# Gate A of a gated decoder block as seven half-size block products, and a layer norm scaled by ScalarE

## The chip, the core and the metric

The kernel runs on one core of one Trainium2 chip. A core has five engines with queues of their own: TensorE (PE) multiplies matrices into PSUM, VectorE (DVE) and ScalarE (ACT) work elementwise, GpSimd (POOL) does elementwise work and issues transfers, SyncE (SP) issues transfers. The metric is device microseconds of one execution; the kernel before takes 796.54 us, the median of three runs (794.74 to 796.85).

## The reference

One decoder block on 512 positions of 1024 channels, all in fp32. What matters here, cut short:

```
z = (rms_norm(x, norm1_g) * (1 + scale1) + shift1) @ w_in      # shift, scale, gate from silu(c) @ w_ada
a_u, a_v, q, k, v, qi, ki, wi, g_a, g_b = split(z)
v    = layer_norm(gelu(a_v), ln_g, ln_b)                       # (4 chunks, 128, 8 groups, 128)
y_a  = gelu(a_u) * (einsum('gts,nsgc->ntgc', tril(w_s), v) + b_s.T)
y_b  = sparse attention: indexer scores from qi, ki, wi; the 128 best keys of each query; softmax
x    = x + gate1 * ((sigmoid(g_a) * (y_a @ w_proj_a) + sigmoid(g_b) * (y_b @ w_proj_b)) @ w_out)
x    = x + gate2 * ((silu(f_g) * f_u) @ w_ffn_out)             # f_g, f_u = split(h2 @ w_ffn_in)
return rms_norm(x, final_norm_g)
```

Gate A is g_a = h @ w_in[:, 4168:5192], a product of 512 x 1024 by 1024 x 1024; projection A is y_a @ w_proj_a.

## The kernel before

Every fp32 product is made of three matmuls in a rounded fp32 format (fp32r): each operand is split into a high part (a copy that rounds) and a low part (the difference), and high x high, high x low and low x high are added in PSUM (L66 to L68). Activations lie transposed, channels on partitions, positions along the free side; h is split once into hT. Weights are streamed in chunks of 128 x 1024 elements (four row blocks by 256 columns): SyncE loads a chunk into one of three raw buffers, ScalarE copies it to one of three hi buffers (L125), and VectorE or GpSimd subtracts to one of three lo buffers (L129; for the u products, gate A and projection A it is GpSimd). get() prepares two chunks ahead of the one that TensorE is at. Into the same stream are put the dots of the modulation: 128 outputs of silu(c) @ w_ada each, a multiply and sum on VectorE over a loaded piece (L199); those of the middle of the kernel share one buffer, mraw.

There is no scheduler: each engine does its instructions in the order in which the program writes them, and semaphores hold an instruction until its operands are there. The order is written as steps. The stages that are touched, with the place of each in time:

- Queries, keys and values (62 to 101 us). q_tasks gives each chunk its side work; at the last but one, ki_stats and ki_norm (L631) normalise the indexer key, TensorE transposes it (L648).
- a_v (to 156 us), then gelu; ws is loaded and masked on VectorE (L834).
- a_u (156 to 205 us) in eight chunks. au_tasks(s) is the side work ahead of chunk s, au_post that behind it: at s = 1 and 2 VectorE scales a_v (L872, L873); from s = 3 TensorE mixes a group (mix_mm) and a step later VectorE adds the bias and multiplies with u (mix_ev: L892, L894), ScalarE and VectorE split the result to yT.
- Gate A and projection A (205 to 294 us), group by group of 256 output columns: two chunks of gate A, whose sigmoid ScalarE writes (ga_evac), two of projection A, whose result VectorE multiplies with it (pa_evac, L974). Between them VectorE works off the top-k of the indexer, 16 rounds of three maxima and three replacements (bg: L698, L702).
- Attention, projection B, output and FFN follow. The FFN is already done by seven half-size block products with summed operands (R: 256 columns); the sums of its weights are made by transfers on GpSimd's queue that add in DRAM.

Of the kernel before, what the change touches and what calls it, by code (L numbers as in the profile page):

```python
# [28 lines left out]
def block_kernel(ctx: ExitStack, tc: tile.TileContext, x, x_t, c_row, positions, w_ada_t, w_first, w_in,  # L29
                 gmlp_ln_g, gmlp_ln_b, gmlp_w_s, gmlp_b_s, w_proj_a, w_proj_b,  # L30
# [44 lines left out]

    def add_w(src, kts, c0, n, lo=None, where=None):
# [8 lines left out]
    def issue(i):  # L85
# [22 lines left out]
    def prep(i):  # L108
# [54 lines left out]
    cols = tiny.tile([128, 80], F32, name="cols")  # L163
    A.dma_start(cols[:, 0:67], small)
# [3 lines left out]
    freq = cols[:, 50:51]  # L168
    bgate = {2: cols[:, 51:59], 5: cols[:, 59:67]}
# [98 lines left out]
    dram = ctx.enter_context(tc.tile_pool(name="dram", bufs=1, space=bass.MemoryType.DRAM))  # L268
# [60 lines left out]
    A.dma_start(ident, consts[:, 0:128])  # L329
# [21 lines left out]
    tiny.tile([128, 96], F32, name="fill")  # L351
# [28 lines left out]
    for cmp, sgn in ((OP.is_gt, -1.0), (OP.is_lt, 1.0)):  # L380
# [7 lines left out]
           "q": mid.tile([128, 2, S], F32, name="tab_q", tag="G3", bufs=1)}  # L388
# [117 lines left out]
    for kt in range(8):  # L506
# [53 lines left out]
    kf = mid.tile([128, 2, S], F32, name="kf", tag="A0", bufs=1)  # L560
# [12 lines left out]
    rqt = [mid.tile([128, S], F32, name="rqt", tag=t, bufs=1) for t in ("P0", "P1", "rq")]  # L573
# [29 lines left out]
    k_hi = mid.tile([128, 2, S], F32R, name="k_hi", tag="k_hi", bufs=1)  # L603
    k_lo = mid.tile([128, 2, S], F32R, name="k_lo", tag="k_lo", bufs=1)

    k_pl = mid.tile([128, 2, 128], F32, name="k_pl")

    def k_b(h):
        split(k_hi[:, h], k_lo[:, h], kf[:, h])
        A.activation(k_pl[:, h], kf[:, h, :128], AF.Copy)  # L610

    v_hi, v_lo = (vmid.tile([128, 4, 256], F32R, name=t, tag=t, bufs=1) for t in ("v_hi", "v_lo"))
    kit = mid.tile([128, 4, 64], F32, name="kit", tag="A1", bufs=1)
# [36 lines left out]
    def ki_a():  # L650
        p = kp[0]
        kr.append(mid.tile([128, S], F32, name="kr", tag="A1", bufs=1))
        A.activation(kr[0], p, AF.Identity, scale=igc, bias=ibc)
        rope_a("ki", kr[0], "i", 128)
# [106 lines left out]
    def idx_mms(n):  # L761
        while iu[0] < 24 and n:
# [5 lines left out]
    QT = {0: [lambda: rows_in(0)],  # L768
          1: [lambda: rows_in(1)],
          2: [lambda: qi_a(0)],  # L770
# [47 lines left out]
    vg = [mid.tile([128, 2, D], F32, name=f"vg{i}", tag=f"P{i}", bufs=1) for i in range(2)]  # L818
    lng = mid.tile([128, D], F32, name="lng", tag="G0", bufs=1)
    lnb = mid.tile([128, D], F32, name="lnb", tag="G1", bufs=1)  # L820
    ws = mid.tile([128, 8, 128], F32, name="ws", tag="A0", bufs=1)
    P.dma_start(lng, rows_bcast(gmlp_ln_g, D))
    P.dma_start(lnb, rows_bcast(gmlp_ln_b, D))
    P.dma_start(ws, gmlp_w_s)
    late = {}

    def load_bs():
        late["bsb"] = mid.tile([128, 8, 128], F32, name="bsb", tag="G3", bufs=1)
# [3 lines left out]
    def ws_mask():  # L832
        late["wmT"] = mid.tile([128, 8, 128], F32, name="wmT", tag="G2", bufs=1)
        V.tensor_tensor(late["wmT"], ws, triu[:, None, :].to_broadcast([128, 8, 128]), op=OP.mult)  # L834

    VT = {0: [lambda: k_b(1)], 2: [lambda: rows_a(1), lambda: rows_b(1)], 4: [lambda: rows_a(2), lambda: rows_b(2)], 6: [load_bs], 7: [ws_mask]}
# [51 lines left out]

    def mix_ev(m):
# [1019 lines left out]
```

## Time and profile before

| | |
|---|---|
| median of 3 runs | 796.54 us |
| the profiled execution | 795.69 us, of which the span is 793.9 us |
| TensorE busy | 782.8 us, mean granted clock 0.997 |
| VectorE, ScalarE, GpSimd busy | 649.7, 424.9, 176.4 us |
| moved by DMA | 144.59 MB, mean 182 GB/s |

An engine's busy time is the sum of its instructions' spans; matmuls overlap in their pipeline, so that TensorE's pace is read from the distance between starts. What bounds the kernel is read from the list of waits and from the chain of waits: the work that ended last, followed back step by step to what released it.

### The profile page before, as it was taken

The page shows a single profiled execution, that of the slowest core. Times are in us where ns is not written, and L with a number is a line of the kernel's source. Part 1 is how long each engine was busy: PE and PEld are TensorE (multiplying, and loading weights), DVE is VectorE, ACT ScalarE, POOL GpSimd, SP SyncE. Part 2 cuts the span into 40 slices and gives each one's busy share as a digit, 9 for nine tenths or more (in the row PEclk, how much of TensorE's full clock was granted, in tenths as well). Part 3 has the DMA queues.
Part 4 walks back from the last instruction along what each step waited for, and adds up shares of the span by engine and source line. Part 5 has one row for each costly group of instructions (what it writes and reads, how often), then busy time and mean ns, then how long its engine had stood idle before and what let it go on. Part 6 is the DMA issues. An engine that isn't in the chain of part 4 may idle for free.

```text
span 793.9 us, 12210 instructions
## 1 busy us (share of the span) xinstructions
PE 782.8 (99%) x4599; PEld 692.8 (87%) x4599; DVE 649.7 (82%) x1093; ACT 424.9 (54%) x757; POOL 176.4 (22%) x206
## 2 busy tenths in 40 slices
PE   8999999999999999999999999999999999999996
PEld 6779988888888888988888899999999999878885
DVE  5985865798899748886697879889999898798887
ACT  6555545423322237665536577555655656576654
POOL 2062224362353411000020000313231222100001
PEclk9999999999999999999999999999999999999998
DMA  9946353432346551148682503989897978565754
GB/s 362 416 155 169 112 191 82 126 92 94 131 150 203 180 186 54 54 133 270 226 244 52 190 1 108 248 256 276 248 273 208 261 192 215 173 200 199 226 182 148
DMA packets 87148, 144.59 MB, mean 182 GB/s; under 512 B 6705, under 2 KB 54593, under 8 KB 86898
## 3 DMA queue, kind: packets, MB, share of 16 engines
q1 hardware_dynamic: 75328, 112.97, 43.1%
q0 software_dynamic: 10864, 29.83, 16.1%
q10 hardware_dynamic: 898, 1.03, 0.4%
q8 instruction: 36, 0.59, 0.3%
q14 instruction: 22, 0.18, 0.1%
HBM read 139.73 MB, written 25.17 MB: 208 GB/s over the span
## 4 chain that ended last, share of the span: by engine, by line
PE 85%; DVE 8%; ACT 3%; DMA 2%; issue 1%; POOL 0%; POOLq 0%; SPq 0%; ACTq 0%; DVEq 0%
PE pb L68 8%; PE pb L67 8%; PE pb L66 8%; PE R L66 7%; PE R L67 7%; PE R L68 7%; PE pfo L67 4%; PE pfo L66 4%; PE pfo L68 4%; PE pgb L66 2%; PE pgb L67 2%; PE pgb L68 2%; PE pav L67 2%; PE pav L66 2%; PE pav L68 2%
## 5 line engine op out<-in xcount | busy, mean ns | idle before, releaser
L125 ACT ACTIVATE hi<-raw 128x1024 fp32r<-128x1024 f32 (+1 forms) x105 | 107.9, 1029 | 90.0 <-PE pb L67 24.2
L129 DVE TENSOR_TENSOR lo<-raw,hi 128x1024 fp32r<-128x1024 f32 (+2 forms) x69 | 80.6, 1169 | 27.9 <-ACT hi L125 27.8
L129 POOL TENSOR_TENSOR lo<-raw,hi 128x1024 fp32r<-128x1024 f32 x29 | 72.8, 2513 | 99.3 <-ACT hi L125 67.9
L66 PE MATMUL pb<-h,hi 128*128 128x512 f32 (+1 forms) x176 | 67.4, 383 | 0.0
L68 PE MATMUL pb<-h,lo 128*128 128x512 f32 (+1 forms) x176 | 66.8, 379 | 0.0
L67 PE MATMUL pb<-h,hi 128*128 128x512 f32 (+1 forms) x176 | 66.8, 379 | 0.0
L67 PE MATMUL pfo<-lo,za 128*128 128x512 f32 (+1 forms) x144 | 55.5, 385 | 0.5 <-DVE lo L129 0.5
L66 PE MATMUL pfo<-hi,za 128*128 128x512 f32 (+1 forms) x144 | 55.4, 384 | 0.0
L68 PE MATMUL pfo<-hi,za 128*128 128x512 f32 (+1 forms) x144 | 55.2, 384 | 0.0
L199 DVE CUSTOM_DVE_ANT_0 mraw<-mraw,scb,cols 128x1024 f32<-128x1024 f32 x27 | 39.3, 1456 | 14.6 <-DMA mraw<-in_w_ada_t_dram 14.6
L321 POOL COPY sm<-sm 128x1 f32<-128x1 f32 x36 | 27.5, 763 | 86.3 <-ACT sm L320 86.3
L66 PE MATMUL R<-tb,sx 128*128 128x256 f32 x160 | 44.7, 280 | 0.3 <-ACT R L1647 0.3
L66 PE MATMUL R<-tb,hi 128*128 128x256 f32 x160 | 44.4, 278 | 0.0
L67 PE MATMUL R<-tb,hi 128*128 128x256 f32 x160 | 44.4, 278 | 0.0
L68 PE MATMUL R<-tb,lo 128*128 128x256 f32 x160 | 44.4, 278 | 0.0
L68 PE MATMUL R<-tb,sx 128*128 128x256 f32 x160 | 44.4, 277 | 0.0
L67 PE MATMUL R<-tb,sx 128*128 128x256 f32 x160 | 44.4, 277 | 0.0
L68 PEld LDWEIGHTS pb<-h,lo 128*128 128x128 f32 x176 | 33.0, 188 | 5.7
L66 PEld LDWEIGHTS pb<-h,hi 128*128 128x128 f32 x176 | 33.1, 188 | 5.5
L67 PEld LDWEIGHTS pb<-h,hi 128*128 128x128 f32 x176 | 33.1, 188 | 5.4
L301 POOL DMA_DIRECT2D wsum<-in_w_ffn_out_dram x24 | 21.3, 889 | 68.7 <-DMA wsum<-wsum 34.7
L67 PEld LDWEIGHTS pfo<-lo,za 128*128 128x128 f32 x144 | 27.1, 188 | 6.6 <-DVE lo L129 1.4
(374 smaller groups left out, 2553.7 us busy)
## 6 DMA issues: line engine op xcount, KB each, us to landing
raw<-in_w_ffn_in_dram SPq DMA_DIRECT2D x44, 512.0 KB, 5.6
raw<-in_w_in_dram SPq DMA_DIRECT2D x38, 512.0 KB, 3.7
wsum<-in_w_ffn_out_dram POOLq DMA_DIRECT2D x30, 512.0 KB, 7.8
mraw<-in_w_ada_t_dram SPq DMA_DIRECT2D x27, 512.0 KB, 3.6
raw<-wsum SPq DMA_DIRECT2D x20, 512.0 KB, 3.7
s<-in_w_ada_t_dram SPq DMA_DIRECT2D x16, 512.0 KB, 8.8
raw<-in_w_ffn_out_dram SPq DMA_DIRECT2D x16, 512.0 KB, 4.4
wsum<-wsum POOLq DMA_DIRECT2D x10, 512.0 KB, 5.3
```

Source lines behind the costliest of these rows:

```text
L66: T.matmul(o, wh, rh, start=start, stop=False, **kw)
L67: T.matmul(o, wh, rlo, start=False, stop=False, **kw)
L68: T.matmul(o, wlo, rh, start=False, stop=stop, **kw)
L125: A.activation(hi[:, :m], e["raw"][:, :m], AF.Copy)
L129: e["lo"].tensor_sub(lo[:, :m], e["raw"][:, :m], f(hi[:, :m]))
L199: V.tensor_tensor_reduce(out=raw[:, o], in0=raw[:, o], in1=c, scale=1.0, scalar=col if o.start else bias, op0=OP.mult, op1=OP.add, accum_o ...
L301: P.dma_start(wsum[n][o], src, accum_op=OP.add)
L321: P.tensor_copy(t, t)
```

## The change

1. Gate A is done in two rounds of 512 output columns. Each is a 2 x 2 block product, (positions halves) x (row halves) times (row halves) x (column halves), made of seven block products of 256 positions, 512 rows and 256 columns instead of eight. Four of the seven need sums of blocks of h (S1 = A21 - A22, S2 = A11 - S1, S3 = S2 - A22, S4 = A12 - S2), and four need sums of blocks of the weights. VectorE makes these sums of h in place in xT, ScalarE and VectorE split them to buffers of their own (h_hi, h_lo). The weight sums are made in DRAM by sixteen transfers on GpSimd's queue, half of them adding (x_move), spread over the query, a_v and a_u chunks. Results are gathered in PSUM: ScalarE seeds one bank from another with a changed sign, or keeps a bank in SBUF, and VectorE adds the kept ones. All low halves of these weights are GpSimd's. Projection A is as before; two groups follow each round.
2. The layer norm of a_v: ScalarE scales (v - mean) * rstd in one pass; the weight ln_g moves into the mixing's evacuation (one pass of VectorE with a scalar), the offset ln_b into the mixing's bias, for which TensorE sums the columns of the mixing weights and VectorE adds eight products of 128 x 128. The mask is put on by GpSimd.
3. Side work moves: the key's split goes to step 27 of 30, the top-k's rounds get a table by step (BG), six of the dots stand among the block products, two stand in each group of projection A, ScalarE's high half of y goes behind the chunk (ylate) and VectorE's low half ahead of the next (ylow). Several tiles change their place in SBUF, and the scratch of software transfers is halved.

```
+    for r in range(2):
+        W_X.append([])
+        for p, b in enumerate((blk(r, 0), xsum[r, 1], xsum[r, 2], blk(r, 3), xsum[r, 3], blk(r, 2), xsum[r, 4])):
+            W_X[r].append(add_w(b, [0, 1, 2, 3], 0, 256, P, 16))
+            if (r, p) in GA_DOTS:
+                add_m(*next(mm_), mid="A2")
+        for g in (2 * r, 2 * r + 1):
+            W_PA.append(group(w_pa, 256 * g, mods=mm_, pool=2, nm=(1, 1)))
...
-          7: [ki_stats, ki_norm],
-          8: [lambda: k_b(0)]}
+          7: [ki_stats, lambda: h_hi("S1"), lambda: h_lo("S1"), lambda: h_lo("S4"), ki_norm]}
...
     def ln_v2(tk):
         v = vg[tk // 2][:, tk % 2]
-        V.scalar_tensor_tensor(v, v, mva[:, tk, 0:1], lng, op0=OP.subtract, op1=OP.mult)
-        V.scalar_tensor_tensor(v, v, rva[:, tk:tk + 1], lnb, op0=OP.mult, op1=OP.add)
+        A.activation(v, v, AF.Identity, scale=rva[:, tk:tk + 1], bias=nmr[:, tk:tk + 1])
...
     def mix_ev(m):
-        V.tensor_tensor(y.rearrange("p (a n) -> p a n", a=4), p.rearrange("p (a n) -> p a n", a=4),
-                        late["bsb"][:, m, None, :].to_broadcast([128, 4, 128]), op=OP.add)
+        V.scalar_tensor_tensor(y.rearrange("p (a n) -> p a n", a=4), p.rearrange("p (a n) -> p a n", a=4),
+                               lngc[:, m:m + 1], late["bsb"][:, m, None, :].to_broadcast([128, 4, 128]),
+                               op0=OP.mult, op1=OP.add)
         V.tensor_mul(y, y, u)
-        split(yT[m][0], yT[m][1], y)
+        def hi():
+            A.activation(yT[m][0], y, AF.Copy)
+            ylow.append(lambda: V.tensor_sub(yT[m][1], y, f(yT[m][0])))
+        ylate.append(hi)
...
+    def xround(r, evac):
...
+        for p, (key, z, start) in enumerate(X_STEPS):
+            hi, lo = get(W_X[r][p])
+            au_tasks()
+            if start:
+                Z[z] = two(bank(z, "zx"))
+            parts = [(j, m, slice(128 * m, 128 * m + 128), h_block(key, j)) for j in range(4) for m in range(2)]
+            for j, m, cc, (hh, hl) in parts:
+                T.matmul(Z[z][:, m], hi[:, j, cc], hh, start=start and j + m == 0, stop=False, skip_group_check=True)
+                T.matmul(Z[z][:, m], hi[:, j, cc], hl, start=False, stop=False, skip_group_check=True)
+            for j, m, cc, (hh, hl) in parts:
+                T.matmul(Z[z][:, m], lo[:, j, cc], hh, start=False, stop=j == 3, skip_group_check=True)
+            if p == 0:
+                seed_(1, 0)
+            elif p == 1:
+                keep_(3)
+            elif p == 2:
+                seed_(2, 1)
+                zlate.append(lambda: V.tensor_add(Z[1], Z[1], kept[3]))
+            elif p == 3:
+                evac(0, Z[0])
+            elif p == 4:
+                keep_(2)
+                zlate.append(lambda: (V.tensor_sub(Z[3], Z[3], kept[2]), evac(3, Z[3])))
...
+    for r in range(2):
+        xround(r, ga_evac(r))
+        for g in (2 * r, 2 * r + 1):
+            opt_b(W_PA[g], 8, yT, ((0, 1), (2, 3), (0, 1), (4, 5))[g], pa_evac(g), au_tasks, au_post)
```

The first place is VectorE's queue at the indexer key (mv and kin are its mean and normalised form, v_lo the values' low half, hs the splits of the sums of h). Before:

```order
L625 BN_AGGR mv<-bst 128x2
L633 TENSOR_SCALAR kin<-kit,mv,sm 128x128 x4
L637 TENSOR_TENSOR v_lo<-pv_793,v_hi 128x256
L637 TENSOR_TENSOR v_lo<-pv_794,v_hi 128x256
L637 TENSOR_TENSOR v_lo<-pv_795,v_hi 128x256
L637 TENSOR_TENSOR v_lo<-pv_796,v_hi 128x256
```

And now:

```order
L696 BN_AGGR mv<-bst 128x2
L676 TENSOR_TENSOR hs<-xT_109,hs 128x1024
L676 TENSOR_TENSOR hs<-xT_110,hs 128x512
L676 TENSOR_TENSOR hs<-xT_110,hs 128x256 x2
L704 TENSOR_SCALAR kin<-kit,mv,sm 128x128 x4
L708 TENSOR_TENSOR v_lo<-pv_811,v_hi 128x256
```

Four low-part passes of S1 and S4 now stand between the key's statistics and its normalisation.

The second place is ScalarE's queue where gate A begins (hi<-raw is the copy of a weight chunk, y the high half of the mixed product, u the gelu of a_u, sg the sigmoid, zx a PSUM bank of the block products, zk a kept one). Before:

```order
L932 ACTIVATE u<-pb 128x512 x2
L363 ACTIVATE y_1506<-y 128x512
L125 ACTIVATE hi<-raw 128x1024
L363 ACTIVATE y_1507<-y 128x512
L125 ACTIVATE hi<-raw 128x1024
L964 ACT_TABLE_LOAD
L964 ACTIVATE sg<-pb 128x512 x2
```

And now:

```order
L1049 ACTIVATE u<-pb 128x512 x2
L981 ACTIVATE y_1532<-y 128x512
L134 ACTIVATE hi<-raw 128x1024
L1105 ACTIVATE zx<-zx 128x512
L981 ACTIVATE y_1532<-y 128x512
L134 ACTIVATE hi<-raw 128x1024
L1109 ACTIVATE zk<-zx 128x512
L981 ACTIVATE y_1533<-y 128x512
L134 ACTIVATE hi<-raw 128x1024
L1105 ACTIVATE zx<-zx 128x512
```

A high half of y stands ahead of each weight copy, as before, but the chunk that the copy is for now feeds half as many columns, and seeding and keeping a bank are added between.

The third place is VectorE's queue between projection A's first and second product with the gate (part is the product, mraw and GG the dots, sco and m the top-k). Before, these stand around the first:

```order
L199 ISA mraw,GG_88<-mraw,scb,cols 128x1024
L199 ISA GG_88 128x1
L974 TENSOR_TENSOR part_1901<-pb,sg 128x512 x2
L702 MATCH_REPLACE sco_637<-m_2064,sco_637 128x512
L702 MATCH_REPLACE sco_636<-m_2066,sco_636 128x384
L702 MATCH_REPLACE sco_635<-m_2068,sco_635 128x256
```

And now, around the second:

```order
L209 ISA mraw,GG_88<-mraw,scb,cols 128x1024
L209 ISA GG_88 128x1
L773 MATCH_REPLACE sco_640<-m_2325,sco_640 128x512
L773 MATCH_REPLACE sco_639<-m_2327,sco_639 128x384
L773 MATCH_REPLACE sco_638<-m_2329,sco_638 128x256
L209 ISA mraw,GG_88<-mraw,scb,cols 128x1024
L209 ISA GG_88 128x1
L1087 TENSOR_TENSOR part_2316<-pb,sg 128x512 x2
```

Seven dots stand in VectorE's queue from the fifth block product of round 0 up to the second product with the gate (five of them ahead of the first); before, one stood ahead of each chunk of gate A and of projection A alike, from the a_u chunks on.

## Rows read from the trace of the kernel before

**Rows 1.** The page: TensorE's busy time; the chain of waits by engine.
```profile
PE 782.8 (99%) x4599; PEld 692.8 (87%) x4599; DVE 649.7 (82%) x1093; ACT 424.9 (54%) x757; POOL 176.4 (22%) x206
...
PE 85%; DVE 8%; ACT 3%; DMA 2%; issue 1%; POOL 0%; POOLq 0%; SPq 0%; ACTq 0%; DVEq 0%
```
**Rows 2.** Waits of TensorE: us in total, times, longest us.
```profile
PE warm L462 <- POOL ones L352: 2.3, 1, 2.3
PE pfo L67 <- DVE lo L129: 0.5, 2, 0.3
```
**Rows 3.** Busy us by stage: PE, PEld, DVE, ACT, POOL, clock, DMA share, GB/s.
```profile
62.00:101.00 39.00, 39.00 (x229) 37.52 (x229) 29.83 (x58) 20.03 (x40) 9.14 (x15) 1.00 0.53 143
...
205.00:294.00 89.00, 89.00 (x403) 73.87 (x402) 69.25 (x151) 24.92 (x31) 34.16 (x15) 1.00 0.56 183
```
**Rows 4.** Timeline of TensorE, 512 columns and mixing: start us, duration us.
```profile
203.42 0.39 PE L66 MATMUL pb<-h,hi 128*128 128x512 f32 x1
203.65 0.39 PE L67 MATMUL pb<-h,hi 128*128 128x512 f32 x1
...
204.10 1.05 PE L886 MATMUL mix<-wmT,vg 128*128 128x128 f32 x8
204.91 0.48 PE L66 MATMUL pb<-h,hi 128*128 128x512 f32 x1
```
**Rows 5.** Timeline of TensorE in the FFN: first and last of twelve.
```profile
539.31 0.28 PE L67 MATMUL R<-h,sx 128*128 128x256 f32 x1
...
540.56 0.28 PE L66 MATMUL R<-tb,sx 128*128 128x256 f32 x1
```
**Rows 6.** Timeline of all engines at the indexer key.
```profile
95.62 2.39 POOL L129 TENSOR_TENSOR lo<-raw,hi 128x1024 fp32r<-128x1024 f32 x1
95.67 3.19 DVE L633 TENSOR_SCALAR kin<-kit,mv,sm 128x128 f32<-128x128 f32 x4 [1.46 <-POOL sm L360]
...
98.78 1.41 DVE L637 TENSOR_TENSOR v_lo<-pv,v_hi 128x256 fp32r<-128x256 f32 x4
...
100.83 0.60 PE L648 MATMUL kiT<-ident,kin 128*128 128x128 f32 x4
```
**Rows 7.** Timeline of GpSimd and VectorE where they meet.
```profile
146.60 2.46 POOL L129 TENSOR_TENSOR lo<-raw,hi 128x1024 fp32r<-128x1024 f32 x1 [5.98 <-ACT hi L125]
...
147.92 2.23 DVE L834 TENSOR_TENSOR wmT<-ws,triu 128x1024 f32<-128x1024 f32 x1
...
160.45 3.25 DVE L873 SCALAR_TENSOR_TENSOR vg<-vg,sm,lnb 128x1024 f32<-128x1024 f32 x1
```
**Rows 8.** Groups by line and shape: busy us, mean ns of one, idle before.
```profile
L873 DVE SCALAR_TENSOR_TENSOR vg<-vg,sm,lnb 128x1024 f32<-128x1024 f32 x4 | 11.1, 2785 | 0.2
L125 ACT ACTIVATE hi<-raw 128x1024 fp32r<-128x1024 f32 x96 | 101.3, 1057 | 84.3 <-PE pb L67 24.2 <-PE pfo L68 11.5 <-issue 11.1
L1331 DVE TENSOR_TENSOR raw<-raw 128x1024 f32<-128x1024 f32 x20 | 24.5, 1226 | 0.7
L894 DVE TENSOR_TENSOR y<-y,u 128x512 f32<-128x512 f32 x8 | 5.5, 692 | 0.3
L363 ACT ACTIVATE y<-y 128x512 fp32r<-128x512 f32 x8 | 5.1, 632 | 28.4 <-DVE y L894 28.4
L364 DVE TENSOR_TENSOR y<-y,y 128x512 fp32r<-128x512 f32 x8 | 5.5, 693 | 5.6 <-ACT y L363 5.6
```
**Rows 9.** Timeline of VectorE: three dots that follow each other.
```profile
243.55 1.28 DVE L199 CUSTOM_DVE_ANT_0 mraw<-mraw,scb,cols 128x1024 f32<-128x1024 f32 x1 [0.60 <-DMA mraw<-in_w_ada_t_dram]
...
248.26 1.33 DVE L199 CUSTOM_DVE_ANT_0 mraw<-mraw,scb,cols 128x1024 f32<-128x1024 f32 x1 [0.45 <-DMA mraw<-in_w_ada_t_dram]
...
253.27 1.72 DVE L199 CUSTOM_DVE_ANT_0 mraw<-mraw,scb,cols 128x1024 f32<-128x1024 f32 x1 [0.69 <-DMA mraw<-in_w_ada_t_dram]
```
**Rows 10.** Transfers by tensor: issues, KB each, median us to landing.
```profile
raw<-in_w_ffn_in_dram SPq DMA_DIRECT2D x44, 512.0 KB, 5.6
raw<-in_w_in_dram SPq DMA_DIRECT2D x38, 512.0 KB, 3.7
```

More of the change, by code (lines that the diff above doesn't have):

```diff
@@ L98, in issue @@
             return
+        if e["where"] == 16:
+            e["view"] = lambda t: t.rearrange("p (j n) -> p j n", j=4)
+            SY.dma_start(raw, e["src"])
+            return
         k0, nk, n = e["kts"][0], len(e["kts"]), e["n"]
@@ new lines, in h_sum, with h_home, four @@
+    def h_sum(key):
+        a, b = {"S1": ("A21", "A22"), "S2": ("A11", "S1"), "S4": ("A12", "S2"), "S3": ("S2", "A22")}[key]
+        V.tensor_sub(h_part(key), h_part(a), h_part(b))
+    def h_home(key):
+        def four(tag, pool=mid):
+            return [(pool.tile([128, 4, 256], F32R, name="hs", tag=tag, bufs=1), 0, 4)]
+        if key == "S1":
+            return four("G0"), four("G1")
+        if key == "S2":
+            return four("G3"), four("gate", base)
+        if key == "S3":
+            return four("G2"), four("k_lo")
+        return four("hs4", base), [(mid.tile([128, 2, 256], F32R, name="hs", tag="rq", bufs=1), 0, 2)] + [
+            (mid.tile([128, 1, 256], F32R, name="hs", tag="qh", bufs=2), 2 + e, 1) for e in range(2)]
@@ new lines, in h_hi, with h_lo, h_block @@
+    def h_hi(key):
+        HS[key] = h_home(key)
+        A.activation(HS[key][0][0][0], h_part(key), AF.Copy)
+    def h_lo(key):
+        hi = HS[key][0][0][0]
+        for t, j, n in HS[key][1]:
+            V.tensor_sub(t, h_part(key)[:, j:j + n], f(hi[:, j:j + n]))
+    def h_block(key, j):
+        if key[0] == "A":
+            o = slice(256 * (key[1] == "2"), 256 * (key[1] == "2") + 256)
+            return tuple(t[:, o] for t in hT[4 * (key[2] == "2") + j])
+        return tuple(next(t[:, j - a] for t, a, n in part_ if a <= j < a + n) for part_ in HS[key])
@@ L901, in au_post @@
     def au_post():
-        for m in AT.get(austep[1], []):
+        s = austep[1]
+        austep[1] += 1
+        if s == 2:
+            rs_mm()
+        for m in AT.get(s, []):
             mix_mm(m)
-        austep[1] += 1
+        while ylate:
+            ylate.pop(0)()
     def au_tasks():
@@ L913, in au_tasks @@
             rstd(rva, mva[:, :, 1], 4, 1.0)
-            run_bg(0.8)
-        elif s == 1:
-            ln_v2(0)
-            ln_v2(1)
-        elif s == 2:
-            ln_v2(2)
-            ln_v2(3)
+            V.scalar_tensor_tensor(nmr, mva[:, :, 0], -1.0, rva, op0=OP.mult, op1=OP.mult)
+        elif s < 3:
+            ln_v2(2 * s - 2)
+            ln_v2(2 * s - 1)
+        elif s == 3:
+            bias_mix()
+        while ylow:
+            ylow.pop(0)()
         for m in AT.get(s - 1, []):
             mix_ev(m)
-        if s > 2:
-            run_bg(1.6 if s < 8 else 2.0)
-        if s in (20, 21):
-            at_split(s - 20)
+        while zlate:
+            zlate.pop(0)()
+        for _ in range(BG.get(s, 0)):
+            run_bg(0.1)
+        if s < 8:
+            x_move()
+        elif s == 8:
+            assert not xm
+        elif s == 27:
+            k_b()
+        if s in (28, 29):
+            at_split(s - 28)
+    BG = {1: 1, 2: 2, 3: 2, 4: 2, 5: 1, 6: 2, 7: 2, 9: 1, 10: 1, 11: 1, 12: 1, 13: 1, 14: 1, 15: 2, 16: 1, 17: 2, 18: 1,
+          19: 1, 20: 1, 21: 1, 22: 1, 23: 1, 24: 1, 26: 2, 27: 1, 28: 1, 29: 1}
+    zlate = []
     def au_evac(g):
@@ L970, in ev @@
         def ev(pb):
+            if not part:
+                part.extend(mid.tile([128, 4, S], F32, name=f"part{i}", tag=f"P{i}", bufs=1) for i in range(2))
             def mul():
@@ new lines, in ga_evac, with ev @@
+    def ga_evac(r):
+        t = {}
+        def ev(z, zb):
+            c, th = z % 2, z // 2
+            if c not in t:
+                t[c] = mid.tile([128, 2, S], F32, name="sg", tag=f"A{c}", bufs=1)
+                for m in range(2):
+                    sig[4 * r + 2 * c + m] = t[c][:, m]
+            A.activation(t[c][:, :, 256 * th:256 * th + 256], zb, AF.Sigmoid)
+        return ev
+    for r in range(2):
+        xround(r, ga_evac(r))
+        for g in (2 * r, 2 * r + 1):
+            opt_b(W_PA[g], 8, yT, ((0, 1), (2, 3), (0, 1), (4, 5))[g], pa_evac(g), au_tasks, au_post)
@@ L1137, in o_w @@
         else:
-            ow[key] = tuple(base.tile([128, 2, S], F32R, name=t, tag=t, bufs=3) for t in ("hi", "lo"))
+            ow[key] = pair((2, S))
         split(*ow[key], oraw[src])
```

168 lines of the change are left out of this document (109 added, 59 removed).

## The prediction

> **What bounds the kernel now.** I read the page first: TensorE is busy in 99% of the span and carries 85% of the chain of waits [rows 1]. The list of waits on TensorE comes next: after the first microseconds its longest sum is 0.5 us [rows 2], and none falls into the stages that are changed. The table of stages says the same: TensorE is busy in all of 62 to 101 us (queries, keys) and of 205 to 294 us (gate A and projection A), at full clock, while VectorE stands at 76 and 78% of those stretches, ScalarE at 51 and 28, GpSimd at 23 and 38 [rows 3]. So a column taken from TensorE is time gained, and any new wait of TensorE is time lost; the two must be set against each other.
>
> **The change part by part.**
>
> *TensorE's columns.* Matmuls of 512 columns start every 0.227 us: three in 0.68 us [rows 4]. Those of 256 columns start every 0.114 us: eleven intervals in 1.25 us [rows 5]. Their listed durations (0.39 and 0.28) overlap and are not to be summed. Gate A goes from 4 groups x 8 row blocks x 2 x 3 = 192 of the first kind, 43.5 us, to 2 rounds x 7 products x 24 = 336 of the second, 38.2 us: -5.3 us. The new column sums of the mixing weights are two plain fp32 matmuls of 512 columns; four of 128 columns take 0.81 us in the mixing [rows 4], so two of 512 take 1.6 to 1.8. Net: -3.6 us.
>
> *The layer norm of a_v.* VectorE loses eight passes over 128x1024, the second four at 2.8 us each [rows 8], and a mask; ScalarE gets four passes, VectorE eight small ones. All of it lies beside the u products, where TensorE waits for nobody: 0 now, 0 then. If ScalarE's four held up a weight copy, that would cost at most one such copy, 1.06 us [rows 8].
>
> *The adding transfers.* Sixteen issues on GpSimd's queue, one every second or third chunk, all before gate A. The queue waits inside a move for the one before it, and the low halves of the weights stand behind it; the chunks of the u products last 5.4 us and GpSimd needs 2.4 of them. I take 0, at most 2 us. The smaller scratch for software transfers has no row; 0, at most 2.
>
> *The sums of h and their splits.* VectorE gets four sums and four differences of 1024 elements, 1.2 us each [rows 8], most of them in the stretch 62 to 101, where 9 us are free [rows 3]. One place is tight. The transposes of the indexer key start at 100.83 and the passes that they wait for end at 98.78 + 1.41 = 100.19 [rows 6]: 0.6 us in hand. The low halves of S1 and S4 are now queued on VectorE ahead of those passes (the first order excerpt). S1's has to wait for a ScalarE copy and ends at about 96.6; then GpSimd's weight piece, 2.39 us long, takes its turn and S4's pieces (1024 elements, 1.3 us) come after it, as the four normalisations did before (3.19 us for four that need 0.8, [rows 6]). So 96.6 + 2.4 + 1.3 + 0.8 + 1.0, where the third of the value passes frees the bank: 102.1, a wait of 1.3 us. Bounds: 0 if GpSimd's turn comes last, 3.7 with one more turn.
>
> *VectorE and GpSimd shut each other out.* GpSimd's weight piece started at 146.60; an elementwise product of two SBUF tensors on VectorE, issued at 147.92, took 2.23 us, which is the rest of GpSimd's piece plus its own length; later a pass with scalars took 3.25 us in the same way [rows 7]. Passes that read one tensor (the top-k's) overlap with GpSimd freely. That decides the new gate A, where GpSimd makes every low half. The Trainium skill, "SBUF — State Buffer", section "Who interferes with whom", has it as a rule: a VectorE instruction with two SBUF inputs and a GpSimd instruction that reads SBUF lock each other out, whoever is first runs alone. The rows above agree with it. By this rule every product and difference of the y passes is shut out too, and the sum is the forecast's; by the narrow reading of the rows (long passes only) it is the second rival's. No run here shows a 512-element product beside GpSimd.
>
> *Round 0 of gate A.* A block product lasts 24 x 0.114 = 2.73 us, half a chunk of before, and still needs a full weight piece: 2.39 us on GpSimd. In its first products the last y passes are unfinished, and they form a ring, since ScalarE's queue holds the high half of y ahead of the next weight copy (second excerpt): low half of the weights 2.39, then (shut out until here) product with u 0.69, high half of y 0.63, weight copy 1.06, next low half: 4.8 us a turn; 6.1 where a y difference (0.69) and a mixing pass (about the same) stand in it too [rows 8]. Three turns at about 5.5. With the third piece done 4.7 us into the round (copies 0.6 + 0.6 + 1.06, low half 2.4), the sixth is done at 21.2; TensorE wants it at 5 x 2.73 + 1.8 = 15.4 (the low half is used in a product's last third). Price: 5.8 us. Bounds: 0 without the exclusion (2.39 fits into 2.73), 10.4 with three long turns and two dots shut out as well. Nothing else hides it: three weight buffers are two products of head start, already counted.
>
> *Round 1.* The dots of the modulation (one each for 128 output columns) share one buffer; they follow each other at 4.7 to 5.0 us, load included [rows 9]. Before, a chunk of 5.4 us paced them. Now seven of them lie ahead of projection A's second product with the gate on VectorE (third excerpt), and the second block product of round 1 needs that bank. From the first of the seven to the end of that product: 6 x 4.9 + 1.3 + 1.3 = 32.0 us; TensorE's own work up to there: 3 x 2.73 + 4 x 5.44 + 2.73 = 32.7. In step, that just fits. But the first dot stands behind the late y passes, near 21 us instead of 10.9, while TensorE is 5.8 late: 10.1 - 5.8 - 0.7 = 3.6. I take 3, bounds 0 and 6.
>
> **Sum.** -3.6 + 1.3 + 5.8 + 3.0 = +6.5 us. The profiled execution took 795.69 us (793.9 of span, 1.8 around it): 802.2. It lies 0.85 below the median of the runs, so I put the median after at **803.0 us**, slower by 0.8%.
>
> **The rivals.**
>
> *The cover holds.* GpSimd's turns fall between VectorE's passes, and the weights arrive in time as they do before. For it: not one wait in these stages before [rows 2]. Against it: step length halves while the weight work per step does not. Only the columns count then: 796.5 - 3.6 = 792.9, faster. It decides as soon as the waits stay under 3.6 us together; below 1.2 they leave it measurable.
>
> *Short passes pass GpSimd by.* Then the ring is gone and so is the late key; the dots stay, some 1.5 us at the end of round 0 and 3 at round 1: 796.5 - 3.6 + 4.5 = 797.4, no change that can be told. For it: only long passes are seen to be stretched.
>
> *The transfers are late.* Three raw buffers turn in load, copy and low half: with 3.7 us for a load [rows 10] (0.4 + 3.7 + 1.06 + 2.39) / 3 = 2.5, under 2.73; with 5.6, as loads take where the DMA engines are full [rows 10], 3.15, which is 0.42 over for 14 pieces: 6 us on top of the forecast, 809. Gate A would ask for 0.5 MB every 2.73 us, about 190 GB/s, plus the dots; before it moved 183 with a DMA share of 0.56 [rows 3].
>
> **How the numbers follow.** Forecast 0.48 (its own range, by the bounds, 798 to 808), the cover holds 0.13, short passes 0.18, late transfers 0.21. What can be told from no change is 0.3%, 2.4 us: faster is below 794.1, slower above 798.9. The cover is faster (0.11 of its 0.13); short passes give two thirds no change; the forecast's lower edge adds a little to that: faster 0.12, same 0.16, slower 0.72. The range reaches from 795, which leaves out most of the cover, to 811, above which a tenth of the late transfers and of the upper bounds lies.
>
> **What would show it.** Right: TensorE's list of waits has new rows: the transposes of the key behind VectorE near 101 us (1 to 2 us), gate A's block products behind GpSimd's low halves and VectorE, projection A behind ScalarE (5 to 8 in sum), and one of some 3 us at the start of round 1; y products and y differences of 512 elements that take over 1 us beside GpSimd; the 256-column matmuls of gate A at 0.114 us where nothing is waited for. Wrong: no waits of TensorE between 60 and 300 us and an end 3.6 us earlier, or waits behind loads.

## The result, and the profile after

The changed kernel takes 806.81 us (median of 4 runs, 805.40 to 807.71), the kernel before, run beside it, 796.69: a ratio of 1.013, 95% interval 1.0106 to 1.0154. It is slower by 10.1 us. 803.0 was forecast, with a range of 795 to 811. The profiled execution took 807.39 us, of which the span is 805.7.

The page of the changed kernel, busy times and the chain of waits by engine [rows 1]:

```profile
PE 785.3 (97%) x4747; PEld 700.5 (87%) x4747; DVE 657.5 (82%) x1106; ACT 442.9 (55%) x777; POOL 208.0 (26%) x228
...
PE 71%; DVE 15%; DMA 5%; ACT 5%; issue 3%; POOL 1%; SPq 0%; POOLq 0%; ACTq 0%; DVEq 0%
```

TensorE's share of the chain fell from 85 to 71%; VectorE's rose from 8 to 15, the transfers' from 2 to 5. The list of waits says where (us in total, times, longest) [rows 2]:

```profile
PE zx L1118 <- DVE part L1087: 3.0, 1, 3.0
PE pb L66 <- ACT sg L1149: 2.8, 1, 2.8
...
PE kiT L719 <- DVE v_lo L708: 1.5, 1, 1.5
...
PE zx L1118 <- DVE zx L1128: 0.9, 1, 0.9
PE pb L68 <- POOL lo L138: 0.7, 1, 0.7
```

Five waits between 60 and 300 us that weren't there before, 8.9 us in all: in the order of time the key (1.5), then round 0 (0.9, 0.7, 2.8), then round 1's second block product (3.0). Something else shows in the table of stages (busy us of PE, PEld, DVE, ACT, POOL, then the granted clock, DMA share, GB/s) [rows 3]:

```profile
236.00:240.00 4.00, 3.82 (x11) 3.02 (x12) 2.20 (x3) 2.50 (x4) 2.85 (x2) 0.62 0.67 234
240.00:244.00 4.00, 4.00 (x18) 3.29 (x17) 4.00 (x13) 1.06 (x1) 3.03 (x2) 0.95 0.56 171
...
264.00:265.00 1.00, 0.01 (x1) 0.04 (x1) 1.00 (x3) 0.44 (x1) 0.48 (x1) 0.65 0.41 49
264.00:268.00 4.00, 3.01 (x14) 3.04 (x15) 3.14 (x6) 0.44 (x1) 2.38 (x1) 0.54 0.80 291
268.00:272.00 4.00, 4.00 (x24) 4.00 (x24) 3.36 (x11) 1.52 (x2) 0.00 (x0) 0.61 0.82 291
```

Right behind each of the two long waits the clock stands near its lower level (1.2 of 2.4 GHz). What that cost is worked out from these rows: 4 x (0.38 + 0.05) = 1.7 us and 4 x (0.46 + 0.39) = 3.4 us. Of the 3.4, 0.35 passed while TensorE still waited (0.65 from 264 to 265, and the wait ends at 264.99), so that 3.1 are left, 4.8 us together. The expectations of e1 and e2 reckon with 5.1, without that deduction. No step of the prediction had it.

Stage by stage, from where gate A and attention begin in the changed kernel:

```profile
208.63 0.36 PE L1118 MATMUL zx<-h,hi 128*128 128x256 f32 x1
...
306.23 0.39 PE L66 MATMUL qk<-k_hi,qh 128*128 128x512 f32 x1
```

and where attention began before:

```profile
294.01 0.39 PE L66 MATMUL qk<-k_hi,qh 128*128 128x512 f32 x1
```

Gate A and projection A lasted 294.01 - 204.91 = 89.1 us [rows 4] and now last 97.6: +8.5. The columns' part is read from the fourth and the fifth block product, between which TensorE waits for nothing:

```profile
218.98 0.28 PE L1118 MATMUL zx<-h,hi 128*128 128x256 f32 x1
...
221.81 0.28 PE L1118 MATMUL zx<-hs,hi 128*128 128x256 f32 x1
```

That is 2.83 us for 24 matmuls, 0.118 us each, where the FFN's started every 0.114 [rows 5]; why the pace differs isn't shown. Fourteen such products are 39.6 us, 3.9 less than the 43.5 of before and not 5.3. So the +8.5 is made of -3.9 for the columns, +7.4 for the waits, +4.8 for the clock and 0.2 that is left over. The key's transposes start 1.95 us later (102.78 against 100.83 [rows 6]; 0.2 of it from the first stages), a_u ends another 1.8 later (the column sums). At the end of the span 11.8 of the 12.2 us are left; that is the difference of these two executions, and the medians differ by 10.1.

### The profile page after: what moved, and what is told of

Same layout as the page of the kernel before. It is cut to its first block, busy times and chain, and to the rows that moved or that the text cites. A ratio compares the mean times of both kernels' runs of the same rounds, so it can differ in the third digit from the quotient of the medians.

```text
span 805.7 us, 12604 instructions
## 1 busy us (share of the span) xinstructions
PE 785.3 (97%) x4747; PEld 700.5 (87%) x4747; DVE 657.5 (82%) x1106; ACT 442.9 (55%) x777; POOL 208.0 (26%) x228
## 4 chain that ended last, share of the span: by engine, by line
PE 71%; DVE 15%; DMA 5%; ACT 5%; issue 3%; POOL 1%; SPq 0%; POOLq 0%; ACTq 0%; DVEq 0%
PE R L66 7%; PE R L68 7%; PE R L67 7%; PE pb L68 5%; PE pb L67 5%; PE pb L66 5%; PE pfo L67 3%; PE pfo L66 3%; PE pfo L68 3%; DMA mraw<-in_w_ada_t_dram 3%; PE pgb L66 2%; PE pgb L68 2%; PE pgb L67 2%; PE pav L67 2%; PE pav L66 2%
## 5 line engine op out<-in xcount | busy, mean ns | idle before, releaser
L134 ACT ACTIVATE hi<-raw 128x1024 fp32r<-128x1024 f32 (+1 forms) x111 | 114.4, 1031 | 75.0 <-PE pb L67 29.1
L138 POOL TENSOR_TENSOR lo<-raw,hi 128x1024 fp32r<-128x1024 f32 x35 | 90.5, 2591 | 88.5 <-ACT hi L134 62.2
L209 DVE CUSTOM_DVE_ANT_0 mraw<-mraw,scb,cols 128x1024 f32<-128x1024 f32 x26 | 37.5, 1442 | 23.5 <-DMA mraw<-in_w_ada_t_dram 23.5
L354 POOL COPY sm<-sm 128x1 f32<-128x1 f32 x36 | 29.5, 819 | 79.5 <-ACT sm L353 79.5
L66 PE MATMUL pb<-h,hi 128*128 128x512 f32 (+1 forms) x112 | 42.7, 381 | 0.0
L68 PE MATMUL pb<-h,lo 128*128 128x512 f32 (+1 forms) x112 | 41.9, 374 | 0.0
L67 PE MATMUL pb<-h,hi 128*128 128x512 f32 (+1 forms) x112 | 41.9, 374 | 0.0
L66 PEld LDWEIGHTS pfo<-hi,za 128*128 128x128 f32 x144 | 27.1, 188 | 5.9 <-ACT ps L1924 0.6
L68 PEld LDWEIGHTS pfo<-hi,za 128*128 128x128 f32 x144 | 27.1, 188 | 5.2
L1399 POOL TENSOR_TENSOR sm<-sm,mhalf 128x1 f32<-128x1 f32 x7 | 4.6, 661 | 100.7 <-DVE sm L1398 100.7
```

Of the source, the lines that this page charges most:

```text
L66: T.matmul(o, wh, rh, start=start, stop=False, **kw)
L67: T.matmul(o, wh, rlo, start=False, stop=False, **kw)
L68: T.matmul(o, wlo, rh, start=False, stop=stop, **kw)
L134: A.activation(hi[:, :m], e["raw"][:, :m], AF.Copy)
L138: e["lo"].tensor_sub(lo[:, :m], e["raw"][:, :m], f(hi[:, :m]))
L209: V.tensor_tensor_reduce(out=raw[:, o], in0=raw[:, o], in1=c, scale=1.0, scalar=col if o.start else bias, op0=OP.mult, op1=OP.add, accum_o ...
```

## The experiments

Each ratio is against runs of the kernel before on the same chip, made beside it. Unless the text says otherwise an edit is one on the changed kernel.

| run | edit | us | before | ratio (95%) |
|---|---|---|---|---|
| e1 | two buffers for the dots | 796.76 | 794.88 | 1.0027 (1.0015 to 1.0039) |
| e2 | dead matmuls in the two long waits | 805.88 | 794.88 | 1.0148 (1.0116 to 1.0179) |
| e3 | banks of its own for projection A | 803.39 | 794.88 | 1.0118 (1.0099 to 1.0137) |
| e4 | S1's and S4's low halves behind the key | 805.07 | 794.88 | 1.0143 (1.0122 to 1.0165) |
| e5 | before, with the layer norm's part alone | 797.82 | 795.91 | 1.0025 (1.0010 to 1.0039) |
| e6 | e1, round 0's low halves on VectorE | 803.37 | 795.91 | 1.0098 (1.0083 to 1.0113) |
| e7 | e1, mixing earlier | 794.22 | 795.91 | 0.9984 (0.9971 to 0.9997) |
| e8 | e7, low halves of S1 and S4 in a_v | 794.76 | 795.91 | 0.9979 (0.9966 to 0.9992) |
| e9 | e8, one adding transfer later | 793.46 | 796.44 | 0.9968 (0.9947 to 0.9988) |
| e10 | that transfer alone | 805.34 | 796.44 | 1.0125 (1.0095 to 1.0156) |
| e11 | e9 with e3 | 793.93 | 796.44 | 0.9974 (0.9955 to 0.9994) |

**The two long waits: e1, e3.** The trace of the changed kernel lets each be followed back. Timeline (start, duration, in brackets the idle time before it and what ended it), first the wait of 2.8 us, then that of 3.0:

```profile
226.84 1.43 DVE L209 CUSTOM_DVE_ANT_0 mraw<-mraw,scb,cols 128x1024 f32<-128x1024 f32 x1
228.30 0.34 SPq L205 DMA_DIRECT2D mraw<-in_w_ada_t_dram  x1
233.10 1.28 DVE L209 CUSTOM_DVE_ANT_0 mraw<-mraw,scb,cols 128x1024 f32<-128x1024 f32 x1 [3.24 <-DMA mraw<-in_w_ada_t_dram]
234.31 0.69 DVE L1133 TENSOR_TENSOR zx<-zx,zk 128x512 f32<-128x512 f32 x1
235.04 1.08 ACT L1149 ACTIVATE sg<-zx 128x512 f32<-128x512 f32 x2 [6.39 <-DVE zx L1133]
236.18 0.50 PE L66 MATMUL pb<-y,hi 128*128 128x512 f32 x1 [2.77 <-ACT sg L1149]
...
262.24 1.39 DVE L209 CUSTOM_DVE_ANT_0 mraw<-mraw,scb,cols 128x1024 f32<-128x1024 f32 x1 [2.12 <-DMA mraw<-in_w_ada_t_dram]
263.56 1.28 DVE L1087 TENSOR_TENSOR part<-pb,sg 128x512 f32<-128x512 f32 x2
264.99 0.55 PE L1118 MATMUL zx<-hs,hi 128*128 128x256 f32 x1 [2.99 <-DVE part L1087]
```

The load of a dot is issued when the dot before it has freed the one buffer, and lands 4.8 us later. VectorE stands still for it (3.24 us), and behind it stand the correction of a bank, ScalarE's sigmoid and TensorE. The second chain is the same, with the product with the gate behind the dot.

e1 gives the dots a second buffer, and lets a load be issued while one dot and two weight chunks are still ahead of it, where before it was no dot and one chunk. The two were not tried apart.

```
-            raw = mid.tile([128, 1024], F32, name="mraw", tag=e["mid"], bufs=1)
+            tag = e["mid"]
+            if tag == "A2":
+                mrot[0] += 1
+                tag = ("A2", "A3")[mrot[0] % 2]
+            raw = mid.tile([128, 1024], F32, name="mraw", tag=tag, bufs=1)
...
+        if e["kind"] == "m" and e["mid"] == "A2":
+            return sum(p["kind"] == "m" for p in pend) <= 1 and sum(p["kind"] == "w" for p in pend) <= 2
```

> The dots among the block products and projection A take turns in two buffers (the second in the place of the mixing's bias, free by then), so that a load starts while the dot before it is still waiting; nothing else changes. Theory D (the dots' one buffer makes VectorE late, and TensorE's two long waits stand at the end of that): the waits of 2.8 us (projection A behind the sigmoid) and of 3.0 us (block product behind the product with the gate) go, and with them the half clock behind them, 5.1 us by the granted clock of 236 to 244 and 264 to 272 us: about 796 us. Theory G (the ring of GpSimd's low halves and the y passes makes the lateness): the two long waits stay within 1 us of what they are, 804 to 807. Both: the waits of 0.9 and 0.7 us in round 0 stay.

The list of waits of e1, its second dot in round 0, and the low half beside it:

```profile
PE pb L68 <- POOL lo L142: 1.6, 1, 1.6
PE kiT L725 <- DVE v_lo L714: 1.5, 1, 1.5
PE zx L1124 <- DVE zx L1134: 0.9, 1, 0.9
```

```profile
229.41 1.83 DVE L215 CUSTOM_DVE_ANT_0 mraw<-mraw,scb,cols 128x1024 f32<-128x1024 f32 x1
230.11 3.35 POOL L142 TENSOR_TENSOR lo<-raw,hi 128x1024 fp32r<-128x1024 f32 x1
```

The dot waits for nothing now, both long waits are gone, the clock is 1.00 through the stage, and the ratio falls by 0.0103, 8.2 us. Theory D holds: of what the change lost, most hung on one buffer and the order of issue that goes with it. The projection's wait for a low half grew from 0.7 to 1.6: the last of GpSimd's low halves ahead of it took 3.35 us, beside the second dot, which now comes earlier; in the changed kernel it took 2.37.

e3 leaves the dots alone and takes the banks out of the two chains:

```
-            opt_b(W_PA[g], 8, yT, ((0, 1), (2, 3), (0, 1), (4, 5))[g], pa_evac(g), au_tasks, au_post)
+            opt_b(W_PA[g], 8, yT, ((4, 5), (6, 7), (6, 7), (4, 5))[g], pa_evac(g), au_tasks, au_post)
```

> Projection A's four groups use banks 4 to 7, none of which the block products use, so that no block product waits for a product with the gate and no group waits for a sigmoid to free its bank. Theory L (the lateness is VectorE's and ScalarE's, whose queues hold the weight copies behind the same sigmoids and the scores of the dots; a bank only shows it first): the two long waits turn into waits for weight copies and low halves, spread over both rounds; 804 to 808 us in all unless they are so short that the clock holds. Rival B (only the bank is held up): both waits and the half clock go, 796 us.

```profile
PE zx L1118 <- DVE zx L1128: 3.8, 2, 2.9
...
PE pb L68 <- POOL lo L138: 1.6, 2, 0.9
...
PE zx L1118 <- ACT zx L1105: 1.3, 1, 1.3
```

Theory L: the two waits are gone by name, but 6.7 us of others stand in round 0 and 1, with one of 2.9 us and a clock down to 0.67 behind it. The bank only showed the lateness first. The ratio, 1.0118, is not to be told from the changed kernel's.

**The clock: e2.**

```
+    def spin(n):
+        w = bank(7, "spin")
+        for k in range(n):
+            T.matmul(w[:, 0:256], yT[0][0][:, 0:128], yT[0][0][:, 0:256], start=True, stop=True)
...
+            if i == W_PA[0][0]:
+                spin(26)
...
+            if (r, p) == (1, 1):
+                spin(26)
```

> Adds work that nothing reads: 26 matmuls of 256 columns (2.95 us) into a free bank ahead of projection A's first chunk, and 26 ahead of the second block product of round 1, the two places where TensorE waits for 2.8 and 3.0 us. Theory C (the long waits cost twice: first themselves, then the granted clock falls to half for some microseconds): TensorE is busy instead of waiting, the clock stays at 1.00, and the 5.1 us of half clock are won though no wait is served sooner: 801.7 us. Rival (the clock falls for another reason, or falls as well behind such work): 806.8 and the clock of these stretches still near 0.5.

The two stretches and the start of attention in e2 (gate A begins at 208.32):

```profile
236.00:240.00 4.00, 4.00 (x18) 3.30 (x19) 2.22 (x2) 2.20 (x3) 3.16 (x2) 1.00 0.60 218
...
264.00:268.00 4.00, 4.00 (x38) 4.00 (x37) 3.21 (x11) 1.55 (x2) 1.38 (x2) 1.00 0.94 323
```

```profile
302.71 0.39 PE L66 MATMUL qk<-k_hi,qh 128*128 128x512 f32 x1
```

In the stage theory C holds: TensorE was given 5.9 us of dead work, the clock stayed at 1.00, and gate A with projection A lasted 94.4 us instead of 97.6. Other waits of 2.2 us are left, so that dead work and waits come to 8.1 us where the waits were 7.4; of the 4.8 us of the clock 4.1 were then to be won, and 3.2 came. In the time of the whole kernel it isn't shown: the ratio is the changed kernel's within the intervals. In the profiled execution the FFN, from its first block product (R) to the first matmul of its second product (pfo), took 195.8 us against 193.6 in that of the changed kernel. In the other traces it takes 192.1 to 195.4, with nothing changed in it, so that a difference of this size comes from one execution to the next. The clock's cost rests on the rows and on e2's stage.

**The ring of GpSimd's low halves: e6, e7.** The rows of round 0 in the changed kernel that the prediction's ring is made of:

```profile
210.16 2.62 POOL L138 TENSOR_TENSOR lo<-raw,hi 128x1024 fp32r<-128x1024 f32 x1 [5.12 <-ACT hi L134]
211.23 2.09 DVE L978 TENSOR_TENSOR y<-y,u 128x512 f32<-128x512 f32 x1
213.36 0.63 ACT L981 ACTIVATE y<-y 128x512 fp32r<-128x512 f32 x1 [0.98 <-DVE y L978]
213.90 1.04 ACT L134 ACTIVATE hi<-raw 128x1024 fp32r<-128x1024 f32 x1
215.02 2.38 POOL L138 TENSOR_TENSOR lo<-raw,hi 128x1024 fp32r<-128x1024 f32 x1 [2.24 <-ACT hi L134]
215.42 2.54 DVE L978 TENSOR_TENSOR y<-y,u 128x512 f32<-128x512 f32 x1
```

Low half, product, high half, weight copy, low half: 4.9 us from one low half to the next (4.8 was worked out), the product of 0.69 us stretched to 2.1 and 2.5.

```
-            W_X[r].append(add_w(b, [0, 1, 2, 3], 0, 256, P, 16))
+            W_X[r].append(add_w(b, [0, 1, 2, 3], 0, 256, P if r else V, 16))
```

> The kernel with two buffers for the dots, and the seven low halves of round 0's block products made by VectorE instead of GpSimd. Theory X (VectorE's passes with two SBUF inputs and GpSimd's pieces shut each other out): VectorE's products of y with u, 2.1 to 2.5 us long in round 0 now, are 0.7 us again, though VectorE has 7 x 1.17 = 8.2 us more to do and only some 4.5 us to win; TensorE's waits in round 0 change from GpSimd to VectorE and grow, 798 to 801 us. Rival (the products are long for another reason, contention with transfers or ScalarE): they stay over 1.5 us.

```profile
212.33 0.69 DVE L984 TENSOR_TENSOR y<-y,u 128x512 f32<-128x512 f32 x1
...
217.19 0.69 DVE L984 TENSOR_TENSOR y<-y,u 128x512 f32<-128x512 f32 x1
...
226.98 0.36 PE L1124 MATMUL zx<-hs,hi 128*128 128x256 f32 x1 [2.49 <-DVE zx L1134]
```

Theory X: with GpSimd idle the same product takes 0.69 us, and VectorE, now with more to do, is what TensorE waits for (2.5 and 1.8 us, and a clock of 0.79 behind the first). The time, 803.4, is 2 us above what was expected; the clock was not reckoned with there either. "SBUF — State Buffer", section "Who interferes with whom", of the Trainium skill has the lock as a rule; the trace agrees, down to a product of 512 elements (0.69 us with GpSimd idle, 2.1 and 2.5 beside a low half).

```
-    AT = {3: [0], 4: [1, 2], 5: [3], 6: [4], 7: [5], 8: [6], 9: [7]}
+    AT = {3: [0, 1], 4: [2, 3], 6: [4, 5], 7: [6, 7]}
```

> The kernel with two buffers for the dots, and the mixing moved one to two chunks ahead, so that the last y products are made beside the last chunk of a_u and the first block product of round 0 and not up to the third. Theory G (what is left of the waits in round 0, 0.9 + 1.6 us, comes of the ring of y passes and GpSimd's low halves): with fewer y passes in the ring the two waits shrink to about 1 us together; 1 to 2 us faster than with two buffers alone (796.8). Rival R (GpSimd's low halves alone, 2.4 to 2.6 us each with a weight copy of 1.05 ahead, can't keep up with 2.73 us a block product): the waits stay within 0.5 us, each product waiting a little.

Measured: the waits of 0.9 and 1.6 us become one of 0.6, and the ratio falls from 1.0027 to 0.9984, 3.4 us, more than the 1 to 2 expected (where attention begins, e7's trace is 2.2 us ahead of e1's, 294.5 against 296.7). Theory G holds for what e1 left: the ring is worth about 2 us of waits, not the 5.8 that the prediction gave it. This kernel is faster than the changed one, and by 0.16% faster than the one before, with an interval that ends just below 1.

**The key: e4, e8, e9, e10.** In the changed kernel:

```profile
95.48 1.08 POOL L269 DMA_DIRECT2D xsum<-in_w_blocks_dram  x1 [0.46 <-issue]
95.67 1.22 DVE L676 TENSOR_TENSOR hs<-xT,hs 128x1024 fp32r<-128x1024 f32 x1 [0.81 <-ACT hs L671]
...
97.03 1.37 POOL L393 TENSOR_TENSOR sm<-sm,mhalf 128x4 f32<-128x4 f32 x1
98.44 2.42 DVE L704 TENSOR_SCALAR kin<-kit,mv,sm 128x128 f32<-128x128 f32 x1 [0.28 <-POOL sm L393]
...
102.78 0.30 PE L719 MATMUL kiT<-ident,kin 128*128 128x128 f32 x1 [1.55 <-DVE v_lo L708]
```

The prediction had the low halves of S1 and S4 on VectorE. They are there, but they end at 98.17, and the normalisation starts at 98.44 because the inverse deviation, a power that GpSimd works out, ends only then: an adding transfer (1.08 us to issue) stands ahead of it in GpSimd's queue.

```
-          7: [ki_stats, lambda: h_hi("S1"), lambda: h_lo("S1"), lambda: h_lo("S4"), ki_norm]}
+          7: [ki_stats, lambda: h_hi("S1"), ki_norm, lambda: h_lo("S1"), lambda: h_lo("S4")]}
```

> The low halves of S1 and S4 stand behind the key's normalisation on VectorE instead of ahead of it. Theory K (the key's wait is that order alone): the wait of 1.5 us at the key goes and nothing takes its place: 805.2 us. Rival M (VectorE's 2.6 us of passes only move): they now stand ahead of the key's rotation, and GpSimd's turn with them; the wait turns up at the first chunks of a_v, about 1 us long, and the time stays within 0.7 us of 806.8.

Measured: the key still waits 1.0 us, and a_v waits 1.6 at a chunk near 109 us. Neither theory had both; M comes nearer. The ratio is not to be told from the changed kernel's.

```
-        if s in (0, 2, 4, 6):
+        if s in (0, 2, 4):
             x_move()
...
-            if vs % 2:
+            if vs % 2 or vs == 2:
                 x_move()
```

> The changed kernel with that one transfer put a stage later and nothing else, so that the low halves of S1 and S4 still stand ahead of the key on VectorE. The prediction's step (GpSimd's 2.39 us piece takes its turn between S1's pass and S4's three pieces): the key's wait stays at 1 to 1.5 us, now from VectorE's order alone, S4's first piece being stretched to over 2 us. Theory P alone: the wait goes.

e10's VectorE:

```profile
95.08 4.71 DVE L676 TENSOR_TENSOR hs<-xT,hs 128x1024 fp32r<-128x1024 f32 x4 [0.83 <-ACT hs L671]
99.71 0.59 DVE L704 TENSOR_SCALAR kin<-kit,mv,sm 128x128 f32<-128x128 f32 x2
```

Without the transfer the power is ready in time, GpSimd's weight piece (96.06 to 98.56) falls between S1's and S4's passes, the four take 4.71 us instead of 2.50, and the key waits 1.3 us: the prediction's own step, with its number. Two causes stood side by side, each enough for most of the wait (1.3 us in e10, 1.0 in e4). So both have to go: in e8 the low halves move to a_v's second chunk, in e9 the transfer to its third as well.

```
-          7: [ki_stats, lambda: h_hi("S1"), lambda: h_lo("S1"), lambda: h_lo("S4"), ki_norm]}
+          7: [ki_stats, lambda: h_hi("S1"), ki_norm]}
...
+          1: [lambda: h_lo("S1"), lambda: h_lo("S4")],
```

> Two buffers for the dots, the mixing earlier, and the low halves of S1 and S4 taken out of the key's place and put ahead of a_v's second chunk. If the three repairs add up: the key's wait of 1.5 us goes too and a_v does not wait for it; of the waits only about 1 us in round 0 is left, so that the columns saved show: 794.9 before - 3.6 + 1 to 2 = 792.5 to 793.5, faster than before by 0.2 to 0.3%. Rival (VectorE's low-half passes find no free place): a wait of 1 to 1.6 us in a_v, about 795.

> The three repairs, and the adding transfer that GpSimd issued just ahead of the key's statistics put a stage later. Theory P (what is left of the key's wait, 1.0 us, is GpSimd's queue: the transfer's issue, 1.07 us, and the 0.45 us ahead of it stand before the two small operations of the inverse deviation, without which VectorE can't normalise the key): VectorE's normalisation starts near 96 us as before the change (95.67) and not at 97.56, and the key's wait goes; 0.8 to 1 us faster than the three repairs. Rival V (the key is late because its statistics themselves come 0.3 to 0.4 us later and GpSimd's weight piece takes its turn first): the wait stays at 0.5 us or more.

VectorE's normalisation in e8, and in e9:

```profile
97.56 3.19 DVE L710 TENSOR_SCALAR kin<-kit,mv,sm 128x128 f32<-128x128 f32 x4 [3.14 <-POOL sm L399]
```

```profile
96.05 3.21 DVE L710 TENSOR_SCALAR kin<-kit,mv,sm 128x128 f32<-128x128 f32 x4 [1.62 <-POOL sm L399]
```

e8 leaves 1.0 us at the key and none in a_v; e8's time is not to be told from e7's. In e9 the key waits for nothing any more (theory P), and one wait of 0.6 us is all that is left of those of the change. e9 has the lowest ratio, 0.9968; its interval overlaps those of e7, e8 and e11, so that the 0.8 to 1 us expected is shown by the wait and not by the time.

**e11** joins e9 and e3:

> The four repairs, and projection A in banks 4 to 7. Once VectorE and ScalarE are in time, a bank of its own should be worth what is left of waits for banks: 0.4 us at the second block product of round 1 (behind the product with the gate). Theory: 0 to 0.5 us faster than without; rival (the other banks collide with the attention's first scores or the modulation's sums, as when they were tried alone, where the modulation waited 0.5 us for a product): the same time or 0.5 us slower.

No difference that can be told (793.93 and 793.46), though the block products wait for no bank in either.

**The layer norm's part alone: e5**, on the kernel before (ln_v2 by ScalarE, ln_g and ln_b in the mixing, two matmuls for the column sums):

> The kernel before with the change's second part alone: ScalarE scales (v - mean) * rstd, the weight ln_g goes into the mixing's evacuation, the offset ln_b into its bias through two matmuls of 512 columns; gate A, the mask and all other places stay as before. Theory (all but the column sums lies beside the u products): slower by the two matmuls' 1.6 to 1.8 us, 0.2% (about 796.5 where before is 794.9), and no wait of TensorE in 156 to 205 us. Rival (ScalarE's four passes hold up weight copies): a wait of TensorE for a high or low half near 160 to 175 us of up to 1.1 us a pass, 3 to 6 us in all.

1.9 us slower, and no wait of TensorE anywhere from 100 to 300 us: this part costs its two matmuls and nothing else, as reckoned.

## Why the prediction was right, point by point

The direction and the places of the waits were right; the sum, +6.5 us, lay 3.6 us under the 10.1 measured. That the total fell into the range is partly luck: the columns were worth less than reckoned, the clock was missing, and the waits were put a little too high.

- *Columns, -3.6 us.* Mis-sized. The pace of 0.114 us was read in the FFN, and "the 256-column matmuls of gate A at 0.114 us" was to show the forecast right; they start every 0.118. Gate A takes 39.6 us and not 38.2, and with the column sums (1.7 reckoned, 1.9 in e5) the columns are worth some 2 us net. In e9, with all but 0.6 us of the waits gone, attention begins 1.2 us earlier than before (292.8 against 294.0); by its ratio the whole kernel is 2.5 us faster (1.0 to 4.2).
- *Layer norm, adding transfers, scratch, 0.* Right for the layer norm (e5). The transfers were costed at 0 "at most 2", and the worth of the one in front of the key is within that, but the reason given (GpSimd has time to spare) missed that an issue of 1.08 us delays whatever stands behind it. e9 keeps the other transfers and the smaller scratch, and no wait of TensorE between 60 and 300 us points at them.
- *The key, 1.3.* Measured 1.5. The step was right as far as e10 shows it (1.3), but in the changed kernel a second cause came first, which the prediction didn't see.
- *Round 0, 5.8.* Waits of 0.9 + 0.7 + 2.8 = 4.4. The size is near by luck, since the cause is half wrong: the prediction's price was all the ring's. The ring is there (4.9 us a turn), but e1 takes away the 2.8 by the dots' buffer and its order of issue alone; the ring's own share is the 0.9 and up to 1.6 that e7 reduces to 0.6. The step that failed is "three turns at about 5.5" against a need at 15.4: the turns took 4.8 each (third low half done at 212.78, sixth at 227.19), since VectorE's other passes found room between them, and TensorE came to the sixth product later, because two mixing groups of 0.8 us [rows 4] stand in the round that the prediction left out.
- *Round 1, 3.0.* Measured 3.0, by the chain that was given: seven dots on one buffer ahead of the product with the gate. Its terms were off, and that they met is luck: the first dot came 18.2 us into the round and not 21 (226.84 - 208.63), the dots followed each other at 5.9 us and not 4.9 ((262.24 - 226.84) / 6), and TensorE asked for the bank 53.4 us into the round (264.99 - 2.99 - 208.63) and not 49.4 (10.9 + 32.7 + 5.8).
- *What was not in the sum.* The clock, 4.8 us in the profiled execution. TensorE had no long wait in the trace of before, so no row of it showed the price, and the prediction took a wait for its own length. Of the waits themselves the prediction had 1.2 us too much (1.3 + 5.8 + 3.0 against 8.9). With the 1.4 us of the columns that makes 6.5 + 4.8 + 1.4 - 1.2 = 11.5, for 11.8 between the two profiled executions.
- *The rivals.* "The cover holds" fell with the five waits. "Short passes pass GpSimd by" fell with e6. "The transfers are late" fell too: in the changed trace TensorE waits for no weight load; the only load that counts is that of a dot, late by its buffer and not by the engines (e1 moves as much, 155 MB, and its dots wait for none in these stages).

## What to carry to other kernels

Work that is cut from the engine that bounds is worth something only if each step's side work still fits into the shorter step: go through every queue of the step in order, its transfers' issues and its single buffers too, and not through busy shares (VectorE's stayed at 82%). A queue in order makes a wait for a load everybody's wait, so a second buffer for 128 x 1024 elements with an earlier issue was worth 8.2 us here, where the columns had saved some 2. A pace read in another stage is an assumption: the FFN's 0.114 us did not carry over to gate A. And a wait of TensorE of some 3 us can bring the slow clock behind it, so that its price is a range, from its own length to twice that.

## What the runs showed of the hardware

The clock's cost was the surprise. Waits of 2.8 and 3.0 us were followed by 1.7 and 3.1 us lost at the lower level; in e6 a wait of 2.5 us was followed by a fall too, one of 1.8 was not, and neither the key's 1.5 nor the 1.6 in e1 was. These are e6's two stretches (the same columns as above):

```profile
228.00:236.00 8.00, 6.99 (x45) 6.51 (x43) 8.00 (x14) 2.07 (x4) 2.39 (x1) 0.79 0.76 254
236.00:244.00 8.00, 7.25 (x32) 6.02 (x33) 8.00 (x23) 4.13 (x6) 6.20 (x3) 1.00 0.79 260
```

The length of the wait alone does not settle it. e4 changes nothing near gate A and has the same second wait, of 2.99 us, and there the clock stayed at 1.00:

```profile
265.88 0.36 PE L1118 MATMUL zx<-hs,hi 128*128 128x256 f32 x1 [2.99 <-DVE part L1087]
264.00:272.00 8.00, 6.12 (x52) 6.15 (x53) 7.20 (x18) 2.72 (x4) 3.77 (x2) 1.00 0.77 257
```

In e10, whose two long waits are the same again, 2.9 us were lost behind the first and 1.6 behind the second. So the 4.8 us are one execution's; but all four runs of the changed kernel have a mean granted clock of 0.989 to 0.994, and e1's six, without the long waits, one of 0.995 to 0.999. What decides between a fall and none isn't shown here.

The Trainium skill has the two levels, and that an idle TensorE falls to the lower, in "TensorE: Matmul & The Clock Gate", section "Part 1: The HAM clock gate (the "warmup" mystery)"; the trace agrees in five of the six long waits above (2.5 to 3.0 us), not in e4's. It shows what a fall is worth in a kernel that is otherwise at full clock: up to about as much again as the wait.
